# An RWKV-7 and pooling layer on one core: products without a reader, a new order of the first loads, and decayed keys on VectorE

## The chip, the cores and the metric

The kernel runs on one core of one Trainium2 chip. Its engines are TensorE (PE, matrix products; PEld is its weight load), VectorE (DVE), ScalarE (ACT), GpSimd (POOL) and SyncE (SP, which here only issues DMA transfers); each works through its own queue of instructions in order. The metric is the device time of one execution in microseconds, the median of several runs; lower is better. Three runs of the kernel before gave 1648.79, 1649.15 and 1650.57.

## What is computed

One inference step of one layer: 256 new positions of a prompt and 8 sequences of 4 new tokens, 288 columns together, with 2048 channels in float32. In the reference's words, cut:

```python
h = _rmsnorm(x, norm_pre_mix)
z = h @ w_in
zs, zp, zga, zgb = jnp.split(z, ...)
zs_mix = zs + (prev - zs) * mu_shift
ya, new_wkv = _rwkv7_branch(zs_mix, st_wkv, ...)
yb, new_pool = _pool_branch(zp, st_pool, ...)
m = jax.nn.sigmoid(zga) * (ya @ w_branch_a) + jax.nn.sigmoid(zgb) * (yb @ w_branch_b)
x = x + _rmsnorm(m @ w_out, norm_post_mix)
f, new_conv = _conv_ffn(_rmsnorm(x, norm_pre_ffn), st_conv, ...)
x = x + _rmsnorm(f, norm_post_ffn)
# in _rwkv7_branch, per head of 64 channels, per position:
s = s * w_t + sa * b_t + v_t * k_t;   y_t = s @ r_t
```

The recurrence over the positions has 16 heads; its decays w_t, keys k_t and the pair a_t, b_t come from z through small products and nonlinear functions. The outputs are y for both kinds of sequence and the new states (shift, wkv, pool, conv).

## The kernel before, in words

**Layout.** Channels lie on the 128 partitions, the 288 columns on the free axis, so x is 16 slices of 128x288. The big products are made in fp32r with both factors split in two: `scaled_parts` (L354) makes xh on ScalarE (L356) and xl = x·g − xh on VectorE (L357), and each product of a 128x128 block of weights is three matmuls (`three`, L262: whi·xh at L263, whi·xl at L264, wlo·xh at L265).

**The stream of weights.** All weights are cut into units of four blocks (256 KB). SP loads a unit into one of seven `raw` buffers (L187), ScalarE casts it to whi (L202), VectorE subtracts to wlo (L203); whi and wlo have four buffers each. A unit is 12 matmuls. The stream runs through the whole kernel: first the five columns of z with the low-rank inputs and the first branch inputs (`dense_together`, five accumulators over the 16 slices of x side by side, 240 matmuls), then r, k, v, the pooling inputs, the gates and the branch products in an order of stages, then w_out, then the FFN in three thirds.

**The side work.** Between the units, generators do the rest in small steps. Three `Lane` objects each hold a list of them; `advance()` is called at the end of a unit and steps all lanes, `advance(True)` in the middle of a unit and steps lane2 alone. A generator's `yield n` lets n steps pass, and a yielded function is asked at each step until it is true. The 16 heads are done in four groups of two pairs. `front(g)` on lane1 makes a group's decays (cum, eP, eN), AR (the queries, decayed, and the negative keys) and KB (the decayed keys: kq and bb times eN, one multiplication for each and each half of the partitions, L621), and then sets `ready[g]`. `late(g)` on lane2 waits for `ready[g]`, multiplies KB with AR (ps_g), masks the result (Gm), writes a part of it to DRAM and reads it back in another layout (Ab), inverts 32x32 triangles of it on VectorE (`inverse`, from the memset at L725 on), reads the inverse back as W and runs the chain of chunks (ps_x, X, ps_u, UV, ps_s, S). lane3 finishes a group.

**What sets the order.** The instructions of each engine are put in order before the run by a scheduler that simulates the kernel with its own costs; an instruction that is pinned (`pin`) keeps its place among the pinned ones in the order of the program. An engine then works strictly in that order.

**The first microseconds.** ScalarE issues the loads of vec (331 columns of per-channel vectors; the first 16 are the gains g1 of the first norm) and of con (1115 columns of constants: identity, ones, masks, eps). SP issues x in pairs of slices and the first units. `startup()` (L417) on lane1 makes the other 12 slices' parts in pairs and then the squares of x, which POOL adds up (L413), for the first norm. `der` (L447) holds four vectors made from vec.

**The second norm.** `rstd_spread` (L381) sums squares with small products (ps_sum), takes the root on ScalarE and the reciprocal on VectorE, writes it on a diagonal (dg, L392) and spreads it over the partitions with one product (ps_spread, L396). It is called for the norm behind w_out (`rst2`, L1220), whose result scales og; x is updated (L1230) and split into xh and xl for the FFN, which begins right behind it. A second call at the end of the kernel is not touched.

Of the kernel before, what the change touches and what calls it, by code (L numbers as in the profile page):

```python
# [10 lines left out]
F32 = mybir.dt.float32  # L11
# [7 lines left out]
P = 128  # L19
# [22 lines left out]
FA = 2  # L42
TOG = 3
# [64 lines left out]
def hybrid_step(ctx: ExitStack, tc: tile.TileContext, t):  # L108
# [69 lines left out]
    def load_to(u):  # L178
        while cursor["load"] <= min(u, len(units) - 1):
            i = cursor["load"]  # L180
            if i in (4, 4 + 5, 4 + 10):
                x_load((i - 4) // 5 + 1)
            ap, nk = units[i]
            m = ap.shape[2]
            w = wp.tile([P, UK, P], F32, tag="raw", name="raw", bufs=7)
            if i:
                nc.sync.dma_start(out=w[:, :nk, :m], in_=ap)  # L187
            raw[i] = w
            cursor["load"] += 1
# [130 lines left out]
    nc.scalar.dma_start(out=vec, in_=t["vec"])  # L320
# [3 lines left out]
    nc.scalar.dma_start(out=con, in_=t["con"])  # L324
    xr = []

    def x_load(q):
        xq = xr_p.tile([P, 4, N], F32, name=f"xr{q}")
        xr.extend(xq[:, i] for i in range(4))
        if q == 0:  # L330
            load_to(0)
            nc.sync.dma_start(out=xq[:, 0:2], in_=t["xT"][:, 0:2, :])
            nc.sync.dma_start(out=raw[0][:, 0:4], in_=units[0][0][:, 0:4])
            nc.sync.dma_start(out=xq[:, 2:4], in_=t["xT"][:, 2:4, :])
            load_to(1)
        else:
            for h in range(0, 4, 2):
                nc.sync.dma_start(out=xq[:, h:h + 2], in_=t["xT"][:, 4 * q + h:4 * q + h + 2, :])
# [7 lines left out]
    def c_(name):  # L346
        o, w = CON[name]
        return con[:, o:o + w]
# [30 lines left out]
    def rstd_spread(sums, where, between=()):  # L379

        ps = psb.tile([P, 3, 2], F32, tag="s", name="ps_sum")  # L381
        for i, a in enumerate(sums):
            for c in range(3):
                pin(pe.matmul(ps[0:TC, c], a[:, c * TC:(c + 1) * TC], ones[:, 0:2],
                              start=i == 0 and c == 0, stop=i == len(sums) - 1 and c == 2))
            if i < len(between):
                between[i]()
        q = where.tile([TC, 3, 1], F32, tag="rq", name="rq")
# [7 lines left out]
        pin(pe.matmul(pr[:, :N], ones[0:TC], dg.rearrange("p c t -> p (c t)"), start=True, stop=True))  # L396
        return pr[:, :N]
# [6 lines left out]
    def first_parts(k):  # L404
        xh[k], xl[k] = scaled_parts(k, xr[k], v_("g1", k))

    def first_squares(k):
        if k == 0:
            act.activation(out=acc, in_=xr[0], func=AF.Square)
            return  # L410
        sq = xr_p.tile([P, N], F32, tag="sq", name="sq", bufs=3)
        act.activation(out=sq, in_=xr[k], func=AF.Square)
        pool.tensor_tensor(acc, acc, sq, op=ALU.add)  # L413

    def startup():
        for k in range(4, KD, 2):
            first_parts(k)  # L417
            first_parts(k + 1)
            yield
        for k in range(KD):  # L420
            first_squares(k)
            if k % 2:
                yield
        norms["mix"] = rstd_of([acc], "mix", cst)

# [106 lines left out]
    def front(g, rr, kx, vv, lora):  # L532
# [85 lines left out]
        for par in range(2):  # L618
            for eng, src, flip in ((dve, kq, 0), (pool, bb, 1)):
                h, slot = HALF[par], par ^ flip  # L620
                ins = eng.tensor_tensor(  # L621
# [4 lines left out]
                )  # L626
                if eng is dve:
                    pin(ins)
            if not par:
                yield  # L630
# [24 lines left out]
    def late(g):  # L655
# [67 lines left out]
        def inverse():  # L723
            yield 2 * IWAIT
# [270 lines left out]
    act.copy(out=bones_r, in_=c_("bones"))  # L995
# [224 lines left out]
    rst2 = rstd_spread([acc2, sq], ep)  # L1220
# [261 lines left out]
```

## Time and profile before

| | us |
|---|---|
| median of 3 runs | 1649.15 |
| lowest and highest | 1648.79, 1650.57 |
| the profiled execution | 1651.69 |
| its span, first to last instruction | 1649.6 |
| PE busy in it | 1611.8 (98%) |
| DVE, ACT, POOL busy | 1103.4, 816.8, 369.7 |
| PE's mean granted clock | 0.992 of full speed |

The profile is one execution. A row of a timeline has start and length in us, engine, line of the kernel, operation, out<-in by the program's names, shapes and a count, and in brackets the engine's idle time before it with what ended it. Matmuls overlap, so their pace is read from one start to the next, not from a length. A float32 matmul leaves two records, an fp32r one leaves one. Row by row, the starts of PE lie 0.13 us apart for most of the span and 0.24 us apart where the granted clock is half.

### The profile page before, as it was taken

What the parts mean: (1) busy time and instruction counts of PE and PEld (TensorE: products, weight loads), DVE (VectorE), ACT (ScalarE), POOL (GpSimd) and SP (SyncE); (2) the same over time, 40 slices, a digit from 0 to 9 for tenths busy, and PEclk for the clock granted to TensorE, in tenths of its full rate; (3) what the DMA queues carried; (4) which work ended last, traced back from release to release, by engine and by line L of the source; (5) the groups of instructions that cost most, each with busy time, mean ns of one, the idle gap of its engine ahead of it and who ended that gap; (6) DMA issues with size and microseconds to landing.
All of it is one profiled execution on the core that took longest, in us unless ns stands there. A gap on an engine that the chain in (4) does not pass through costs nothing.

```text
span 1649.6 us, 35997 instructions
## 1 busy us (share of the span) xinstructions
PE 1611.8 (98%) x13540; PEld 1577.3 (96%) x13540; DVE 1103.4 (67%) x2217; ACT 816.8 (50%) x1521; POOL 369.7 (22%) x612
## 2 busy tenths in 40 slices
PE   6989999999999999999999999999999999999998
PEld 6989989989989999999899999999999999999998
DVE  6788887888878766645876664446666555666654
ACT  5544445445435445545655554445555433455554
POOL 4574352343332112300211110001111000111111
PEclk9999999999999999999999999999999999999999
DMA  7535546546545648755355555555555555555553
GB/s 241 161 120 165 170 142 200 161 122 190 157 155 181 187 155 288 229 166 190 108 163 167 167 165 167 166 167 165 168 167 166 166 166 167 166 167 167 176 167 108
DMA packets 157230, 278.96 MB, mean 169 GB/s; under 512 B 25584, under 2 KB 32240, under 8 KB 157056
## 3 DMA queue, kind: packets, MB, share of 16 engines
q1 hardware_dynamic: 151104, 259.16, 50.8%
q0 software_dynamic: 5664, 16.77, 2.9%
q8 instruction: 106, 1.74, 0.4%
q10 hardware_dynamic: 288, 0.74, 0.1%
q14 instruction: 68, 0.56, 0.1%
HBM read 262.67 MB, written 13.93 MB: 168 GB/s over the span
## 4 chain that ended last, share of the span: by engine, by line
PE 86%; DVE 4%; DMA 2%; issue 1%; POOL 0%; ACT 0%; SPq 0%; DVEq 0%; POOLq 0%; ACTq 0%
PE acc L265 27%; PE acc L263 27%; PE acc L264 27%; DVE wlo L203 1%; DMA dW<-wt 1%; PE ps_g L671 0%; DVE xl L357 0%; DVE og L1229 0%; PE ps_s L909 0%; DMA W<-dW 0%; PE ps_u L899 0%; PE ps_x L888 0%; PE ps_y L1353 0%; DVE cum L577 0%; DMA raw<-in_w_in 0%
## 5 line engine op out<-in xcount | busy, mean ns | idle before, releaser
L203 DVE TENSOR_TENSOR wlo<-raw,whi 128x512 fp32r<-128x512 f32 x928 | 661.1, 715 | 415.2 <-ACT whi L202 406.7
L202 ACT CAST whi<-raw 128x512 fp32r<-128x512 f32 x928 | 572.0, 620 | 680.6 <-PE acc L264 629.7
L263 PE MATMUL acc<-xh,whi 128*128 128x288 f32 x2736 | 814.3, 298 | 14.5 <-ACT whi L202 8.8
L265 PE MATMUL acc<-xh,wlo 128*128 128x288 f32 x2736 | 811.4, 297 | 7.0 <-DVE wlo L203 7.0
L264 PE MATMUL acc<-xl,whi 128*128 128x288 f32 x2736 | 812.7, 297 | 0.0
L263 PEld LDWEIGHTS acc<-xh,whi 128*128 128x128 f32 x2736 | 517.4, 189 | 17.9 <-ACT whi L202 9.2
L265 PEld LDWEIGHTS acc<-xh,wlo 128*128 128x128 f32 x2736 | 520.2, 190 | 12.0 <-DVE wlo L203 8.9
L264 PEld LDWEIGHTS acc<-xl,whi 128*128 128x128 f32 x2736 | 520.6, 190 | 2.0 <-issue 0.9
L265 PE MATMUL acc<-ah,wlo 128*128 128x288 f32 x704 | 208.7, 296 | 0.0
L263 PE MATMUL acc<-ah,whi 128*128 128x288 f32 x704 | 208.0, 296 | 0.0
L264 PE MATMUL acc<-al,whi 128*128 128x288 f32 x704 | 205.2, 292 | 0.0
L1266 POOL COPY cout<-gt 128x2 f32<-128x2 f32 x44 | 31.1, 706 | 597.2 <-DVE gt L1262 575.9
L264 PEld LDWEIGHTS acc<-al,whi 128*128 128x128 f32 x704 | 134.2, 191 | 0.0
L263 PEld LDWEIGHTS acc<-ah,whi 128*128 128x128 f32 x704 | 132.2, 188 | 0.0
L265 PEld LDWEIGHTS acc<-ah,wlo 128*128 128x128 f32 x704 | 131.9, 187 | 0.0
L1274 POOL TENSOR_TENSOR cv<-cv,rstd_ffn 128x288 f32<-128x288 f32 x44 | 36.2, 823 | 74.5 <-ACT cv L1273 73.6
L732 DVE TENSOR_TENSOR wt<-wt,Ab 128x16 f32<-128x16 f32 (+30 forms) x124 | 51.4, 414 | 1.8
L462 POOL TENSOR_TENSOR df<-zt 128x256 f32<-128x256 f32 (+1 forms) x27 | 22.7, 840 | 91.6 <-DVE zt L460 85.6
L1270 DVE SCALAR_TENSOR_TENSOR cv<-gt,vec,cv 128x255 f32<-128x255 f32 x88 | 43.0, 489 | 0.0
L263 PE MATMUL acc<-ybh,whi 128*128 128x288 f32 x128 | 38.6, 301 | 0.0
L265 PE MATMUL acc<-ybh,wlo 128*128 128x288 f32 x128 | 38.4, 300 | 0.0
L264 PE MATMUL acc<-ybl,whi 128*128 128x288 f32 x128 | 38.1, 298 | 0.0
(308 smaller groups left out, 1539.8 us busy)
## 6 DMA issues: line engine op xcount, KB each, us to landing
raw<-in_w_ffn_in SPq DMA_DIRECT2D x352, 256.0 KB, 3.0
raw<-in_w_in SPq DMA_DIRECT2D x264, 256.0 KB, 3.5
raw<-in_w_ffn_out SPq DMA_DIRECT2D x176, 256.0 KB, 2.7
raw<-in_w_out SPq DMA_DIRECT2D x64, 256.0 KB, 3.0
raw<-in_w_branch_b SPq DMA_DIRECT2D x32, 256.0 KB, 3.2
raw<-in_w_branch_a SPq DMA_DIRECT2D x32, 256.0 KB, 3.9
xr<-in_xT SPq DMA_DIRECT2D x8, 288.0 KB, 5.6
tga<-th POOLq DMA_DIRECT2D x16, 144.0 KB, 3.7
```

The costliest lines, as they stand in the source:

```text
L202: act.copy(out=hi[:, a:b, :m], in_=w[:, a:b, :m])
L203: dve.tensor_tensor(lo[:, a:b, :m], w[:, a:b, :m], hi[:, a:b, :m].bitcast(F32), op=ALU.subtract)
L263: pe.matmul(ps, hi, xh, start=start, stop=False)
L264: pe.matmul(ps, hi, xl, start=False, stop=False)
L265: pe.matmul(ps, lo, xh, start=False, stop=stop)
L462: pool.tensor_tensor(df[:m, :TP], zt[:m, 0:TP], zt[:m, 1:ZB], op=ALU.subtract)
L732: dve.tensor_tensor(tmp[:, :, :n], Wb[:, :, :n], Ab[:, :n, tt].unsqueeze(1).to_broadcast([P, 8, n]), op=ALU.mult)
L1266: pool.tensor_copy(cout[:, f, 0:2], gt[:, TP - 2:TP])
L1270: dve.scalar_tensor_tensor(cv[:, s:TP], gt[:, 0:TP - s], w, cv[:, s:TP], op0=ALU.mult, op1=ALU.add)
L1274: pool.tensor_tensor(cv, cv, rst3, op=ALU.mult)
```

## The change

Four things are done.

*The beginning.* Eleven products of a zeroed 128x128 tile, which nothing reads, stand first on PE. The load of vec brings only its first 16 columns; the rest of it and con are loaded on SP's queue in front of the eighth unit. The first slice of x is loaded alone, before the first unit. `startup()` makes one slice's parts and one slice's square per step, and the squares are pinned, as is the copy of bones.

*The keys.* All four multiplications of KB are on VectorE and pinned, in four steps instead of two, so that `ready[g]` is set two units later.

*The inverse.* Group 0's inverse begins two half steps (one unit) later.

*The second norm.* Five products of constants (ones times the identity, float32, 128 columns) stand behind the sums, and eight behind the spreading product; nothing reads them.

```diff
--- before.py
+++ after.py
@@ -40,6 +40,7 @@
 UK = 4
 AHEAD = 3
 FA = 2
+WARM = 11
 TOG = 3
 BT = 5
 IWAIT = 3
@@ -180,6 +181,9 @@
             i = cursor["load"]
             if i in (4, 4 + 5, 4 + 10):
                 x_load((i - 4) // 5 + 1)
+            if i == 7:
+                nc.sync.dma_start(out=vec[:, KD:], in_=t["vec"][:, KD:])
+                nc.sync.dma_start(out=con, in_=t["con"])
             ap, nk = units[i]
             m = ap.shape[2]
             w = wp.tile([P, UK, P], F32, tag="raw", name="raw", bufs=7)
@@ -317,11 +321,10 @@
     con = cst.tile([P, NCON], F32, name="con")
     xe = ExitStack()
     xr_p = xe.enter_context(tc.tile_pool(name="xr", bufs=1, side="right"))
-    nc.scalar.dma_start(out=vec, in_=t["vec"])
+    nc.scalar.dma_start(out=vec[:, 0:KD], in_=t["vec"][:, 0:KD])
     first = cst.tile([P, 1], F32, name="first")
     dve.memset(first, 0.0)
     act.activation(out=first, in_=first, func=AF.Square)
-    nc.scalar.dma_start(out=con, in_=t["con"])
     xr = []
 
     def x_load(q):
@@ -329,8 +332,9 @@
         xr.extend(xq[:, i] for i in range(4))
         if q == 0:
             load_to(0)
-            nc.sync.dma_start(out=xq[:, 0:2], in_=t["xT"][:, 0:2, :])
+            nc.sync.dma_start(out=xq[:, 0:1], in_=t["xT"][:, 0:1, :])
             nc.sync.dma_start(out=raw[0][:, 0:4], in_=units[0][0][:, 0:4])
+            nc.sync.dma_start(out=xq[:, 1:2], in_=t["xT"][:, 1:2, :])
             nc.sync.dma_start(out=xq[:, 2:4], in_=t["xT"][:, 2:4, :])
             load_to(1)
         else:
@@ -376,7 +380,13 @@
 
     TC = N // 3
 
-    def rstd_spread(sums, where, between=()):
+    def keep_busy(n):
+
+        ps = psb.tile([P, 512], F32, tag="s", name="ps_busy")
+        for _ in range(n):
+            pin(pe.matmul(ps[:, 0:P], ones, ident, start=True, stop=True))
+
+    def rstd_spread(sums, where, between=(), busy=()):
 
         ps = psb.tile([P, 3, 2], F32, tag="s", name="ps_sum")
         for i, a in enumerate(sums):
@@ -385,6 +395,8 @@
                               start=i == 0 and c == 0, stop=i == len(sums) - 1 and c == 2))
             if i < len(between):
                 between[i]()
+        if busy:
+            keep_busy(busy[0])
         q = where.tile([TC, 3, 1], F32, tag="rq", name="rq")
         pin(act.activation(out=q, in_=ps[0:TC, :, 0:1], func=AF.Sqrt, scale=1.0 / D, bias=c_("eps")[0:TC]))
         pin(dve.reciprocal(q, q))
@@ -394,6 +406,8 @@
         ))
         pr = psb.tile([P, 512], F32, tag="s", name="ps_spread")
         pin(pe.matmul(pr[:, :N], ones[0:TC], dg.rearrange("p c t -> p (c t)"), start=True, stop=True))
+        if busy:
+            keep_busy(busy[1])
         return pr[:, :N]
 
 
@@ -406,22 +420,26 @@
 
     def first_squares(k):
         if k == 0:
-            act.activation(out=acc, in_=xr[0], func=AF.Square)
+            pin(act.activation(out=acc, in_=xr[0], func=AF.Square))
             return
         sq = xr_p.tile([P, N], F32, tag="sq", name="sq", bufs=3)
-        act.activation(out=sq, in_=xr[k], func=AF.Square)
+        pin(act.activation(out=sq, in_=xr[k], func=AF.Square))
         pool.tensor_tensor(acc, acc, sq, op=ALU.add)
 
     def startup():
-        for k in range(4, KD, 2):
-            first_parts(k)
-            first_parts(k + 1)
+        for k in range(KD):
+            if k < KD - 4:
+                first_parts(k + 4)
+            first_squares(k)
             yield
-        for k in range(KD):
-            first_squares(k)
-            if k % 2:
-                yield
         norms["mix"] = rstd_of([acc], "mix", cst)
+
+
+    zero = xr_p.tile([P, P], F32, name="zero")
+    pool.memset(zero, 0.0)
+    warm0 = psb.tile([P, 512], F32, tag="s", name="ps_warm")
+    for _ in range(WARM):
+        pin(pe.matmul(warm0[:, :P], zero, zero, start=True, stop=True))
 
     first_parts(0)
     split_to(0)
@@ -615,19 +633,17 @@
         KBs = kp.tile([P, G, 2, 32], F32, tag="KBs", name="KBs")
         rh = kp.tile(W2, F32R, tag="t0", name="rh")
         rl = kp.tile(W2, F32R, tag="t3", name="rl")
-        for par in range(2):
-            for eng, src, flip in ((dve, kq, 0), (pool, bb, 1)):
+        for src, flip in ((kq, 0), (bb, 1)):
+            for par in range(2):
                 h, slot = HALF[par], par ^ flip
-                ins = eng.tensor_tensor(
+                pin(dve.tensor_tensor(
                     KB[h, :, :, slot, :].rearrange("p c g t -> p g c t"),
                     src[h, :, :TP].rearrange("p g (c t) -> p g c t", c=NCH),
                     eN[h, :, :TP].rearrange("p g (c t) -> p g c t", c=NCH),
                     op=ALU.mult,
-                )
-                if eng is dve:
-                    pin(ins)
-            if not par:
-                yield
+                ))
+                if (flip, par) != (1, 1):
+                    yield
         for slot, src in enumerate((kq, bb)):
             pool.tensor_tensor(KBs[:, :, slot, :], src[:, :, TP:], eN[:, :, TP:], op=ALU.mult)
         ready[g] = (vv, AR, KB, KBs, wr, dch, dsm)
@@ -721,7 +737,7 @@
         S0 = kp.tile([P, G, NB, C], F32, tag="S0", name="S0")
         nc.sync.dma_start(out=S0, in_=t["st_wkv"][:, p0:p0 + G])
         def inverse():
-            yield 2 * IWAIT
+            yield 2 * IWAIT + (0 if g else 2)
             pin(dve.memset(Ab.rearrange("p a b -> p (a b)")[:, 0:1024:33], 1.0))
             wt = kp.tile([P, 2, 8, 32], F32, tag="inv", name="wt")
             Wb, tmp = wt[:, 0], wt[:, 1]
@@ -992,7 +1008,7 @@
         lane3.todo.append(finish())
 
     bones_r = zp_.tile([P, P], F32R, name="bones_r")
-    act.copy(out=bones_r, in_=c_("bones"))
+    pin(act.copy(out=bones_r, in_=c_("bones")))
     mB = [dmb.tile([P, N], F32, tag=f"mB{j}", name=f"mB{j}") for j in range(16)]
     tga = [dmb.tile([P, N], F32, tag=f"tga{j}", name=f"tga{j}") for j in range(16)]
 
@@ -1217,7 +1233,7 @@
         act.activation(out=o, in_=ps[:, :N], func=AF.Copy, scale=v_("g2", j))
         og.append(o)
     me.close()
-    rst2 = rstd_spread([acc2, sq], ep)
+    rst2 = rstd_spread([acc2, sq], ep, busy=(5, 8))
     acc3 = ep.tile([P, N], F32, tag="accn3", name="acc3")
     xh, xl = [None] * KD, [None] * KD
```

How this moves the instructions is shown at three places. First VectorE at the start, where xl are the x slices 8 to 15 in their order (L357 before, L361 now) and wlo the weights of the units. Before:

```order
L203 TENSOR_TENSOR wlo<-raw,whi 128x512 x3
L203 TENSOR_TENSOR wlo<-raw,whi 128x4x96
L357 SCALAR_TENSOR_TENSOR xl_233<-xr_111,vec,xh_232 128x288
L357 SCALAR_TENSOR_TENSOR xl_237<-xr_111,vec,xh_236 128x288
L357 SCALAR_TENSOR_TENSOR xl_257<-xr_111,vec,xh_256 128x288
L357 SCALAR_TENSOR_TENSOR xl_261<-xr_111,vec,xh_260 128x288
L357 SCALAR_TENSOR_TENSOR xl_281<-xr_124,vec,xh_280 128x288
L357 SCALAR_TENSOR_TENSOR xl_285<-xr_124,vec,xh_284 128x288
L357 SCALAR_TENSOR_TENSOR xl_305<-xr_124,vec,xh_304 128x288
L357 SCALAR_TENSOR_TENSOR xl_309<-xr_124,vec,xh_308 128x288
L203 TENSOR_TENSOR wlo<-raw,whi 128x512 x4
```

Now:

```order
L207 TENSOR_TENSOR wlo<-raw,whi 128x512
L361 SCALAR_TENSOR_TENSOR xl_291<-xr_113,vec,xh_290 128x288
L361 SCALAR_TENSOR_TENSOR xl_314<-xr_113,vec,xh_313 128x288
L361 SCALAR_TENSOR_TENSOR xl_337<-xr_113,vec,xh_336 128x288
L361 SCALAR_TENSOR_TENSOR xl_362<-xr_113,vec,xh_361 128x288
L207 TENSOR_TENSOR wlo<-raw,whi 128x512 x2
L361 SCALAR_TENSOR_TENSOR xl_387<-xr_126,vec,xh_386 128x288
L361 SCALAR_TENSOR_TENSOR xl_412<-xr_126,vec,xh_411 128x288
L361 SCALAR_TENSOR_TENSOR xl_437<-xr_126,vec,xh_436 128x288
L361 SCALAR_TENSOR_TENSOR xl_462<-xr_126,vec,xh_461 128x288
L207 TENSOR_TENSOR wlo<-raw,whi 128x512
```

Eight xl stood in a row behind four wlo, then four wlo; now two wlo stand behind the first four of the eight xl.

Second VectorE in the second group (g = 1), where AR, KB are made on lane1 (KB at L621 before, L639 now; bb is written on tha) and S and UV belong to the chain of the first group on lane2. Before:

```order
L203 TENSOR_TENSOR wlo<-raw,whi 128x512
L610 TENSOR_TENSOR AR<-rr,eP 128x576
L608 SCALAR_TENSOR_TENSOR AR<-kkr,thw 128x576
L914 TENSOR_TENSOR S<-S,ps_s 128x128
L203 TENSOR_TENSOR wlo<-raw,whi 128x512
L915 TENSOR_TENSOR S<-S,dch 128x128
L203 TENSOR_TENSOR wlo<-raw,whi 128x512
L621 TENSOR_TENSOR KB<-kq,eN 64x2x4x64
L203 TENSOR_TENSOR wlo<-raw,whi 128x512
L621 TENSOR_TENSOR KB<-kq,eN 64x2x4x64
```

Now:

```order
L207 TENSOR_TENSOR wlo<-raw,whi 128x512 x2
L639 TENSOR_TENSOR KB<-kq,eN 64x2x4x64
L930 TENSOR_TENSOR S<-S,ps_s 128x128
L931 TENSOR_TENSOR S<-S,dch 128x128
L207 TENSOR_TENSOR wlo<-raw,whi 128x512
L639 TENSOR_TENSOR KB<-kq,eN 64x2x4x64
L207 TENSOR_TENSOR wlo<-raw,whi 128x512
L858 TENSOR_TENSOR S_1899<-S_1899,ps_st 128x512 x2
L207 TENSOR_TENSOR wlo<-raw,whi 128x512
L639 TENSOR_TENSOR KB<-tha,eN 64x2x4x64
L918 TENSOR_TENSOR UV<-ps_u,wr 64x2x64 x2
L639 TENSOR_TENSOR KB<-tha,eN 64x2x4x64
```

The two halves from bb (KB<-tha) were on POOL and stand on VectorE now, each with a wlo or more in front; the first half from kq stands ahead of S's update, where it stood behind it; AR is made earlier, outside the rows.

Third PE at the second norm. Before:

```order
L265 MATMUL acc<-xh_10011,wlo 128x288
L384 MATMUL ps_sum<-con,acc_10041 96x2 x3
L384 MATMUL ps_sum<-con,sq 96x2 x3
L396 MATMUL ps_spread<-dg,con 128x288
L263 MATMUL acc<-xh_11311,whi 128x288 x6
L264 MATMUL acc<-xl_11312,whi 128x288
L265 MATMUL acc<-xh_11311,wlo 128x288
```

Now:

```order
L269 MATMUL acc<-xh_10027,wlo 128x288
L394 MATMUL ps_sum<-con,acc_10057 96x2 x3
L394 MATMUL ps_sum<-con,sq 96x2 x3
L387 MATMUL ps_busy<-con 128x128 x5
L408 MATMUL ps_spread<-dg,con 128x288
L387 MATMUL ps_busy<-con 128x128 x8
L267 MATMUL acc<-xh_11342,whi 128x288 x6
L268 MATMUL acc<-xl_11343,whi 128x288
L269 MATMUL acc<-xh_11342,wlo 128x288
```

The products of constants stand in the two places between the sums, the spreading product and the FFN's first matmuls; the matmuls behind keep their order.

## The prediction

> **What bounds the kernel now.** I read the page's first part, then what PE waited for, then stretches of the span, then the timelines where PE waited.
>
> ```profile
> span 1649.6 us, 35997 instructions
> PE 1611.8 (98%) x13540; PEld 1577.3 (96%) x13540; DVE 1103.4 (67%) x2217; ACT 816.8 (50%) x1521; POOL 369.7 (22%) x612
> ```
>
> ```profile
> PE acc L263 <- ACT whi L202: 8.8, 1, 8.8
> PE acc L265 <- DVE wlo L203: 7.6, 6, 3.3
> PE acc L263 <- DVE zb L1027: 4.1, 1, 4.1
> PE ps_u L899 <- ACT X L894: 2.8, 1, 2.8
> ...
> PE acc L263 <- ACT xh L356: 1.6, 1, 1.6
> PE acc L263 <- ACT dh L363: 1.4, 1, 1.4
> PE ps_x L888 <- DVE S L915: 1.3, 1, 1.3
> PE ps_s L909 <- DVE UV L902: 1.2, 1, 1.2
> PE ps_spread L396 <- DVE dg L392: 1.0, 1, 1.0
> ```
>
> ```profile
> 100.00:150.00 50.00, 43.66 (x366) 41.73 (x365) 40.81 (x97) 22.35 (x45) 35.91 (x57) 0.90 0.51 146
> 350.00:480.00 130.00, 123.13 (x1284) 116.05 (x1284) 111.84 (x258) 59.89 (x122) 55.77 (x88) 0.97 0.51 155
> 860.00:1649.00 789.00, 785.12 (x5906) 782.08 (x5904) 453.70 (x840) 384.66 (x663) 80.27 (x136) 1.00 0.53 164
> ```
>
> TensorE is the bound: it is idle for 1649.6 − 1611.8 = 37.8 us, and the columns of the second fence (sum, times, longest, us) say on what. In the third fence the columns are busy time of PE, PEld, DVE, ACT and POOL, then PE's granted clock; the last 789 us lose nothing and are not touched. Besides idle time PE loses clock: 0.90 over 50 us is 10 us at half speed. So whatever the change can win is in the waits above and in the slow time behind them; the rest is product after product.
>
> **The beginning.** Timelines of PE, ACT, DVE and POOL, and of the DMA view of the first 20 us the rate in slices of 0.5 us and con's issue (KB, us to landing):
>
> ```profile
> 8.83 0.61 PE L263 MATMUL acc<-xh,whi 128*128 128x288 f32 x1 [8.83 <-ACT whi L202]
> ...
> 12.27 0.30 PE L263 MATMUL acc<-xh,whi 128*128 128x288 f32 x1
> ...
> 25.54 0.29 PE L264 MATMUL acc<-xl,whi 128*128 128x288 f32 x1
> 29.14 0.47 PE L265 MATMUL acc<-xh,wlo 128*128 128x288 f32 x1 [3.30 <-DVE wlo L203]
> ...
> 49.75 0.29 PE L265 MATMUL acc<-xh,wlo 128*128 128x288 f32 x1
> ```
>
> ```profile
> 8.16 0.62 ACT L202 CAST whi<-raw 128x512 fp32r<-128x512 f32 x1 [2.22 <-DMA raw<-in_w_in]
> ```
>
> ```profile
> GB/s 0 0 0 55 96 267 339 300 231 220 213 285 371 399 424 372 363 343 362 385 382 406 386 386 394 389 352 355 384 376 388 415 378 384 400 383 390 369 164 107
> ...
> con<-in_con ACTq DMA_DIRECT2D x1, 557.5 KB, 7.5
> ```
>
> ```profile
> 21.68 6.80 DVE L357 SCALAR_TENSOR_TENSOR xl<-xr,vec,xh 128x288 fp32r<-128x288 f32 x8
> 28.40 2.48 DVE L203 TENSOR_TENSOR wlo<-raw,whi 128x512 fp32r<-128x512 f32 x4
> ```
>
> The clock's two speeds, read where PE changes from one to the other behind the second norm:
>
> ```profile
> 791.96 1.81 PE L263 MATMUL acc<-xh,whi 128*128 128x288 f32 x6 [1.61 <-ACT xh L356]
> 793.57 0.44 PE L264 MATMUL acc<-xl,whi 128*128 128x288 f32 x1
> 793.81 0.44 PE L265 MATMUL acc<-xh,wlo 128*128 128x288 f32 x1
> ...
> 797.64 0.29 PE L264 MATMUL acc<-xl,whi 128*128 128x288 f32 x1
> ```
>
> A product starts 0.24 us after the last at half clock; at full clock 789.00 us hold 5906 of them, 0.13 each: 0.11 lost on each slow one. The first 8.83 to 12.27 are at half clock: 3.44 / 0.24 = 14 products, 1.5 us lost. The 240 products of the first stage end at 49.9. Since 240 at 0.132 are 31.7, this stage spends 18.2 us on other things: 8.8 before the first product, 1.5 of clock, 3.3 of waiting for wlo, 1.5 of clock again behind it, and 3.1 of shorter waits.
>
> What goes: con's 557.5 KB and most of vec no longer stand in front of the first weights. The first product needs 147 KB of x and one 256 KB unit, 0.4 MB, and the queues move 220 to 340 GB/s from 2.5 us on: landed about 4.0 to 4.8, plus the cast of 0.62. The eleven products of zeros are bounded by the transposes L697 (8 records for 4 of them, each 128 columns of f32):
>
> ```profile
> 120.18 1.09 PE L697 MATMUL ps_t<-con,KB 128*128 128x128 f32 x8
> 121.03 0.38 PE L264 MATMUL acc<-xl,whi 128*128 128x288 f32 x1
> ```
>
> 0.85 / 4 = 0.21 each at full clock, twice that at half: started in the first 0.4 to 1.2 us they end between 5.0 and 5.8. First real product: 5.4, so 3.4 earlier, and at full clock: 1.5 more. The eight xl in a row (0.85 each) stand in front of the four wlo at 28.40; in the new order two wlo stand between two fours of xl, so I expect the 3.3 and its clock loss (1.5) to go, of the shorter waits nothing, and 0.7 to come anew from weights not landed yet: 3.3 + 1.5 − 0.7 = 4.1. **Term 1: 3.4 + 1.5 + 4.1 = 9.0**; ends: 3.4 (start alone) and 11.5 (3.4 + 1.5 + 4.8, and 1.8 of the shorter waits). What is late next is der: it waits on VectorE for the rest of vec, behind seven weight units on SP's queue. 3.1 MB at 385 GB/s put that at 10 to 11 us, and four xl and four wlo are ahead of it; at 14 it would stall the fifth wlo, inside the lower end. The two DMAs are issued by SP right ahead of the eighth unit, which is wanted only after 84 products; the squares and the copy of bones, pinned now, run on ScalarE, busy 816.8 of 1649.6. I cost both at nothing; without that cover an issue or a square would be 0.4 us.
>
> On the clock, the Trainium skill ("TensorE: Matmul & The Clock Gate", Part 1) says that a free-running window of about 3.4 us must be busy, and that its phase is not tied to the kernel. The trace agrees with the length: 12.27 − 8.83 = 3.44. By that rule eleven products can end before the window does, and up to 9 real products would still be slow, an estimate of 1.0 us off this term.
>
> **The keys' halves.** VectorE and POOL beside each other, columns start and length:
>
> ```profile
> 233.45 3.48 POOL L621 TENSOR_TENSOR KB<-tha,eN 64x512 f32<-64x512 f32 x2
> ```
>
> ```profile
> 101.41 1.98 DVE L203 TENSOR_TENSOR wlo<-raw,whi 128x512 fp32r<-128x512 f32 x2
> 103.42 1.64 DVE L621 TENSOR_TENSOR KB<-kq,eN 64x512 f32<-64x512 f32 x1
> ...
> 234.22 1.58 DVE L203 TENSOR_TENSOR wlo<-raw,whi 128x512 fp32r<-128x512 f32 x1
> 235.72 1.35 DVE L915 TENSOR_TENSOR S<-S,dch 128x128 f32<-128x128 f32 x1
> 237.00 0.68 DVE L203 TENSOR_TENSOR wlo<-raw,whi 128x512 fp32r<-128x512 f32 x1
> ...
> 357.56 0.68 DVE L621 TENSOR_TENSOR KB<-kq,eN 64x512 f32<-64x512 f32 x1
> 358.47 1.95 DVE L621 TENSOR_TENSOR KB<-kq,eN 64x512 f32<-64x512 f32 x1
> 360.46 1.73 DVE L608 SCALAR_TENSOR_TENSOR AR<-kkr,thw 128x576 f32<-128x576 f32 x1
> ...
> 453.25 1.76 DVE L203 TENSOR_TENSOR wlo<-raw,whi 128x512 fp32r<-128x512 f32 x1
> ```
>
> While POOL multiplies its two halves (3.48), VectorE's wlo takes 1.58 where it takes 0.68 alone, KB 1.95 instead of 0.68. Each of the four groups has such a place, and PE's waits stand right behind. Moving two halves costs VectorE 2 × 0.68 a group and takes the stretching away. By place:
> - 101: wlo 1.98 − 1.36 and KB 1.64 − 0.68 give 1.6 back; the 4.1 wait becomes 2.5. Rows ahead of zb are the same as before. Slow clock follows it for two windows (10 us at half in 100 to 150, three windows of 3.4 us, one of them from the wait at 144); I count a little less than one of the two as gone, 1.3: 2.9.
> - 235: 0.90 and about 1.07 of stretching go, one KB (0.68) now stands ahead of S: 1.3 (all of the wait, 1.3, for 1.29).
> - 362 and 369: 1.27 + 1.0 go, 1.36 comes: 0.9.
> - 454: 1.1 on wlo, 0.5 on others go, one KB comes: 1.0 of the 2.8 wait; clock 0.97 over 130 us is two windows, 2.7 us of products; half of it: 2.3 together.
>
> **Term 2: 7.4**; ends 0 (the added halves take it all back) and 14.0 (waits and clock all gone).
>
> The Trainium skill ("SBUF — State Buffer", section "SBUF: two separate sides") speaks against the price of 0.68: the pair of ports is held for a whole instruction by whichever of VectorE and GpSimd starts first, so a half placed beside what POOL still does would wait for it. The row at 358.47 agrees (1.95). With all eight added halves at 1.95, the term would be 7.4 − 8 × 1.27, below zero; that is the slower rival below.
>
> **Products added beside the second norm; inverse.** PE waits 1.0 for dg, then 1.6 for xh, then runs at 0.24 from 791.96 to 797.3: 22 products. Five products are 5 × 0.21 = 1.06, eight are 1.70: they fill both waits and add about 0.1. **Term 3: 22 × 0.11 − 0.2 = 2.2**; ends 0 (one short idle stretch is enough to lose the clock) and 2.4. The cover is complete: were dg 1 us earlier, they would cost that. Group 0's inverse one unit (12 products, 1.58 us) later has VectorE wait less at its memset, behind which dh and the 1.4 wait stand, with a slow window behind (1.5). But the order has seven wlo between the last Gm and the memset both times, so the memset comes little later against the transfer it waits for. **Term 4: 0.6**, ends −1 and 2.9. Its late end is covered: 53 products (7 us) are left between the lane's last work and its first use.
>
> **Term 5: −3.0.** ready comes two units later, and the stream's order differs at every group: two new waits of the size of those quoted (1.2 to 1.6); ends −6 and 0.
>
> **Sum.** 9.0 + 7.4 + 2.2 + 0.6 − 3.0 = 16.2. The profiled execution took 1651.69 (span 1649.6 and 2.1 around it), so 1635.5; the median of the three runs is 2.5 below that execution: **1633**.
>
> **Rivals.**
> - *The beginning gives only its earlier start* (0.15): weights do not land fast enough, the waits return a few units on. For: the queues move over 340 GB/s from 6 us on, without a pause; against: con's bytes are out of that stretch. 16.2 − 5.6: 1638.5.
> - *The middle gives nothing* (0.15): VectorE is at 111.84 of 130 in 350 to 480 and pays with its own time. 9.0 + 2.2: 1638. With the first, 5.6: 1643.5.
> - *Slower* (0.06): VectorE becomes the engine waited for in all four groups. Eight added halves at 1.95 are 15.6, and each group loses another slow window, 4 × 1.5 = 6: 21.6 against 11.2 from terms 1 and 3, +10.4: 1659.5. It decides from 14.5 us lost, 3.6 a group. Against: the longest row is 1.95 with POOL's halves beside it, and these go.
> - *Nothing* (0.06): the planner's order puts new waits for 11 to 16 us in the place of the gain, or the clock drops at the start as before: 1649.
> - *My forecast's terms* (0.58): 1627 to 1640 is its own range.
>
> Range 1624 to 1645: the low end is terms 1 to 4 near their upper halves (25), the high end both of the first rivals together. A change below 0.2% (3.3 us) can't be told from none. Faster 0.88, same 0.06, slower 0.06.
>
> **What would show it.** First real product at 5 to 6 with 0.13 between starts; the 240th by 39 to 42; no wlo above 1 us in the four groups' places and no wait for S at 235, moved by the gain so far; zb's wait 2.5 or less; 0.13 between starts right behind the second norm; the last 789 us as before. I am wrong if the first stage ends behind 45, or if PE's wait for VectorE between 90 and 470 is not below the 18 or so of now.

## The result, and the profile after

The changed kernel takes 1636.84 us (median of 4 runs, 1634.78 to 1640.18); the kernel before, on the same chip, 1649.86 (1648.79 to 1651.35). The ratio is 0.9922 with a 95% interval of 0.9903 to 0.9942: 13 us faster, between 10 and 16. The forecast was 1633, range 1624 to 1645. The execution profiled took 1636.18, 15.5 less than the one profiled before.

The page's first part, after:

```profile
span 1634.4 us, 36105 instructions
PE 1612.8 (99%) x13588; PEld 1577.4 (97%) x13588; DVE 1101.7 (67%) x2225; ACT 817.1 (50%) x1521; POOL 350.6 (21%) x605
```

PE is busy 1.0 us longer, for 48 records more (24 products without a reader), and idle 21.6 us where it was 37.8. VectorE has eight multiplications more and is busy 1.7 us less: the stretching that POOL's halves caused is gone, though other work of POOL still stretches VectorE (a wlo of 2.45 at 447.75). What PE waits for now (us in total, times, longest):

```profile
PE ps_q L874 <- DVE tq L868: 3.3, 3, 1.6
PE acc L269 <- DVE wlo L207: 3.3, 5, 1.3
PE acc L267 <- DVE zb L1043: 2.8, 1, 2.8
PE acc L267 <- DVE gt L1278: 2.0, 1, 2.0
PE acc L267 <- DVE ybl L1090: 2.0, 1, 2.0
```

The waits for X, S, UV, dg and xh are gone and the one for zb is 2.8 where it was 4.1; the ones for gt and ybl are new.

Where the time went is seen best from the big products themselves: both kernels make the same 11136 of them (tile acc), so the start of the n-th in the trace before less the start of the n-th in another trace is that kernel's lead there, in us. Where the granted clock is half, for a window of 3.4 us or several, I say that PE runs at half clock. Worked out from the rows of the traces, for the changed kernel and four of the experiments below:

| n | start before | changed | beginning alone | keys alone | POOL's halves, 3 pauses | VectorE, 1 pause |
|---|---|---|---|---|---|---|
| 1 | 8.83 | 2.6 | 2.3 | 0.9 | 2.6 | 2.6 |
| 240 | 49.75 | 6.8 | 6.7 | -0.9 | 7.0 | 7.3 |
| 400 | 72.11 | 4.6 | 3.4 | -0.9 | 4.9 | 5.0 |
| 500 | 86.13 | 4.6 | 3.4 | -0.9 | 4.9 | 5.0 |
| 900 | 159.87 | 7.7 | 4.3 | 0.1 | 6.3 | 5.3 |
| 1200 | 204.48 | 10.3 | 4.3 | 3.0 | 8.6 | 4.5 |
| 2000 | 347.31 | 6.9 | 4.1 | -2.0 | 6.6 | -2.9 |
| 2500 | 432.38 | 8.9 | 3.4 | -1.1 | 7.0 | 0.1 |
| 2700 | 477.25 | 15.6 | 9.1 | 5.3 | 14.6 | 3.8 |
| 4700 | 773.42 | 15.5 | 8.9 | 3.8 | 13.5 | 3.7 |
| 4850 | 800.94 | 17.6 | 9.3 | 3.9 | 15.6 | 5.8 |
| 5050 | 829.14 | 19.4 | 8.6 | 5.7 | 17.3 | 7.6 |
| 5200 | 849.08 | 15.1 | 8.6 | 4.7 | 14.6 | 4.8 |
| 11136 | 1634.03 | 15.1 | 8.6 | 4.7 | 14.6 | 4.8 |

Each column is one execution, and executions of one kernel differ by up to 7 us (see the last section), so differences of a few us between columns are not read as results; the medians are. In the changed kernel the beginning gives 6.8 and loses 2.2 of it again by the 400th product, the middle gives 10.9, the second norm 2.1 and the rows behind it 1.8, and the FFN's first gates take 4.3 back. The middle's gain is waits and clock together. Between 90 and 470 us PE waited 16.4 us before and 9.6 now, and ran at half clock for 17.1 us before (from 104.4, 145.4 and 456.0 on) and for 3.4 now (from 337.5 on). The 13.7 us less at half clock are some 6 us (57 products at 0.11, an estimate).

### The profile page after: what moved, and what is told of

It reads as the page before. It is cut to its first block, busy times and chain, and to the rows that moved or that the text cites. A ratio compares the mean times of both kernels' runs of the same rounds, so it can differ in the third digit from the quotient of the medians.

```text
span 1634.4 us, 36105 instructions
## 1 busy us (share of the span) xinstructions
PE 1612.8 (99%) x13588; PEld 1577.4 (97%) x13588; DVE 1101.7 (67%) x2225; ACT 817.1 (50%) x1521; POOL 350.6 (21%) x605
## 4 chain that ended last, share of the span: by engine, by line
PE 90%; DVE 5%; issue 1%; DMA 1%; POOL 1%; ACT 0%; SPq 0%; DVEq 0%; POOLq 0%; ACTq 0%
PE acc L267 28%; PE acc L269 28%; PE acc L268 28%; DVE wlo L207 2%; DVE wt L748 1%; PE ps_g L687 1%; DMA dW<-wt 0%; DVE wt L751 0%; PE ps_s L925 0%; PE ps_u L915 0%; PE ps_y L1369 0%; PE ps_x L904 0%; PE ps_v L723 0%; PE ps_x L905 0%; PE ps_sl L835 0%
## 5 line engine op out<-in xcount | busy, mean ns | idle before, releaser
L1286 DVE SCALAR_TENSOR_TENSOR cv<-gt,vec,cv 128x255 f32<-128x255 f32 (+1 forms) x88 | 43.4, 494 | 0.3 <-ACT cv L1279 0.3
```

The source lines that it names most:

```text
L1286: dve.scalar_tensor_tensor(cv[:, s:TP], gt[:, 0:TP - s], w, cv[:, s:TP], op0=ALU.mult, op1=ALU.add)
```

## The experiments

Each ran in five rounds; a ratio is to the kernel before, run beside it, with its 95% interval.

**1. The beginning alone.** The changed kernel with the other parts undone (of the keys' loops the first lines alone, the words behind # added):

```diff
-        for src, flip in ((kq, 0), (bb, 1)):   # four steps, all on dve
+        for par in range(2):                   # kq on dve, bb on pool, one pause
-            yield 2 * IWAIT + (0 if g else 2)
+            yield 2 * IWAIT
-    rst2 = rstd_spread([acc2, sq], ep, busy=(5, 8))
+    rst2 = rstd_spread([acc2, sq], ep)
```

> The beginning alone (products of zeros, load order, one slice per step), without the keys on VectorE, the later inverse and the products beside the second norm. Theory from the two traces: the 240th product comes 6.8 us earlier as in the changed kernel and about 2 us of that are given back by the 400th, so 4.6 us in all, 1645. Rival, the forecast: 9 us, 1640.5. If it gives under 3.3 the beginning is worth nothing that can be measured.

Measured: 1642.61, 0.9954 (0.9941 to 0.9966): 7.6 us, between the two. The 240th product leads by 6.7. Of the table's 8.6 at the end, 5.8 came between the 2500th and the 2700th: the wait for X at 454 (2.8 before) is down to 0.4 here too, with POOL's halves in place. That is a change of order, not of the engines.

**2. The products beside the second norm alone.** The kernel before with `keep_busy` as in the change and this call:

```diff
-    rst2 = rstd_spread([acc2, sq], ep)
+    rst2 = rstd_spread([acc2, sq], ep, busy=(5, 8))
```

> The kernel before with the five and eight products beside the second norm alone; the order up to that norm is the one of before. Theory from the traces: 2.1 us are won behind the norm (full clock at once) and lost again at the FFN's first gates, where three wlo now stand ahead of gt on VectorE (a wait of 2.0 us with a slow window of 1.5 behind it): between 1649 and 1651, no gain. Rival, the forecast's third term: 2.2 us stay, 1647.5.

Measured: 1649.31, 0.9999 (0.9991 to 1.0008). No gain, as the theory from the traces had it. In its execution 2.1 us of lead come between the 4700th and the 4850th product, and PE waits 2.0 us for gt, as in the changed kernel.

**3. The changed kernel without them.**

```diff
-    rst2 = rstd_spread([acc2, sq], ep, busy=(5, 8))
+    rst2 = rstd_spread([acc2, sq], ep)
```

> The changed kernel without the five and eight products beside the second norm; the order up to the norm is the changed kernel's. Theory: the slow stretch of 2.1 us behind the norm comes back, the wait for gt of 2.0 us goes with its slow window, the sum is nothing: 1636 to 1637, the same as the changed kernel. Rival, the forecast's third term: 2.2 us slower, 1639.

Measured: 1634.41, 0.9911 (0.9897 to 0.9924): not slower than with them. Both runs say the part is worth nothing as it stands. Why is in the timelines of the changed kernel, PE behind the norm and at the first gates:

```profile
774.70 1.95 PE L387 MATMUL ps_busy<-con 128*128 128x128 f32 x16
776.47 1.06 PE L267 MATMUL acc<-xh,whi 128*128 128x288 f32 x6
777.55 0.40 PE L268 MATMUL acc<-xl,whi 128*128 128x288 f32 x1
777.79 0.29 PE L269 MATMUL acc<-xh,wlo 128*128 128x288 f32 x1
777.92 0.30 PE L268 MATMUL acc<-xl,whi 128*128 128x288 f32 x1
...
817.60 0.37 PE L267 MATMUL acc<-xh,whi 128*128 128x288 f32 x1 [2.00 <-DVE gt L1278]
```

and VectorE at those gates, now and then before:

```profile
813.39 1.95 DVE L378 RECIPROCAL rstd_ffn<-rstd_ffn 128x288 f32<-128x288 f32 x1 [0.20 <-ACT rstd_ffn L377]
815.26 1.82 DVE L207 TENSOR_TENSOR wlo<-raw,whi 128x512 fp32r<-128x512 f32 x3
817.00 0.81 DVE L1278 TENSOR_TENSOR gt<-acc,rstd_ffn 128x288 f32<-128x288 f32 x2
```

```profile
827.06 1.95 DVE L374 RECIPROCAL rstd_ffn<-rstd_ffn 128x288 f32<-128x288 f32 x1
830.53 0.46 DVE L1262 TENSOR_TENSOR gt<-acc,rstd_ffn 128x288 f32<-128x288 f32 x1 [1.52 <-PE acc L265]
```

Behind the norm PE runs at 0.13 at once, as forecast (the 2.1 of the table). But with the thirteen products the scheduler puts the FFN's norm product 40 places later (behind 267 of the stage's products, where without them, in run 3, it stands behind 227) and three wlo between the reciprocal and gt. I take it that it counts the thirteen as PE time. Before, gt waited for PE; now PE waits 2.0 us for gt, and a window of half clock follows.

**4. The keys alone.**

```diff
-            for eng, src, flip in ((dve, kq, 0), (pool, bb, 1)):
+        for src, flip in ((kq, 0), (bb, 1)):
+            for par in range(2):
...
+                if (flip, par) != (1, 1):
+                    yield
```

> The kernel before with the decayed keys on VectorE in four steps alone. Theory: the middle's gain (10.9 us between the 500th and the 4700th product in the traces) is mostly this part's, because POOL's long multiplications beside VectorE are gone: 8 to 11 us, 1639 to 1642. Rival, the forecast's terms two, four and five: 5 us, 1645. Rival of those who hold that VectorE only takes over the work: no gain, 1650.

Measured: 1640.08, 0.9945 (0.9932 to 0.9959): 9 us, the first theory's size. But this part changes two things, the engine and the pauses (each `yield` between two halves is one), and the next runs separate them. (The execution profiled took 1646.7, 6.7 above the median; its column in the table is low for that.)

**5. POOL's halves back, pauses kept.** Two halves on POOL as before, three pauses as in the change:

```diff
-                pin(dve.tensor_tensor(
+                ins = (pool if flip else dve).tensor_tensor(
...
+                if not flip:
+                    pin(ins)
```

> The changed kernel with the two halves from bb back on POOL, still in four steps; PE's order differs from the changed kernel's by a few products only. Theory, the two engines stretch each other: VectorE's rows beside POOL's halves take 1.3 to 2 us again, 5 to 9 us slower than the changed kernel, 1642 to 1646. Rival, the order: what wins the middle is that ready comes later and rows stand elsewhere (the beginning alone removed the wait of 3.0 us at 454 too): within 2 us of the changed kernel, 1635 to 1639.

Measured: 1638.36, 0.9930 (0.9916 to 0.9944). The rival holds: 1.5 us from the changed kernel, not to be told apart, and far from 5 to 9. Yet the stretching is there, in the first group's rows of VectorE and POOL:

```profile
98.78 1.64 DVE L639 TENSOR_TENSOR KB<-kq,eN 64x512 f32<-64x512 f32 x1
```

```profile
96.50 3.37 POOL L639 TENSOR_TENSOR KB<-tha,eN 64x512 f32<-64x512 f32 x2
```

KB takes 1.64 beside POOL and 0.70 in the changed kernel at the same place, and the two wlo in front of it 2.35 against 1.40: 1.9 together. Behind them stands zb, for which PE waits 4.6 against 2.8:

```profile
PE acc L267 <- DVE zb L1045: 5.3, 2, 4.6
```

So each stretch is real, but it reaches PE in the first group alone: in the other three KB takes up to 1.16, 1.77 and 1.78, and the list of this run's waits has none for S, X or UV above 0.4.

**9. VectorE's halves, one pause.**

```diff
-                if (flip, par) != (1, 1):
+                if (flip, par) == (0, 1):
                     yield
```

> The changed kernel with all four halves on VectorE but in two half steps with one pause, as before, so that ready comes two units earlier. Theory after the run with POOL's halves in four steps, the order wins: without the pauses most of the middle's gain beyond the engine's 1.5 us goes, 1640 to 1643. Rival, the engine wins: 1636 to 1638.

Measured: 1646.66, 0.9989 (0.9980 to 0.9997): 11 us slower than the changed kernel, and slower than either expected. With runs 1, 5 and the changed kernel this makes four corners (run 1 also lacks two parts that runs 2 and 10 find to be worth nothing):

| ratio to before | bb's halves on POOL | all on VectorE |
|---|---|---|
| one pause | 0.9954 (0.9941 to 0.9966) | 0.9989 (0.9980 to 0.9997) |
| three pauses | 0.9930 (0.9916 to 0.9944) | 0.9922 (0.9903 to 0.9942) |

With one pause, moving the halves to VectorE costs 0.0035, 6 us; the intervals are apart. With three pauses the engine makes no difference that is measured. The pauses are worth 0.0067, 11 us, on VectorE; with the halves on POOL they come out at 0.0024, 4 us, with intervals that overlap, so nothing is shown there. What they do: `ready` is set two units later and the halves are spread, so that one KB stands between two wlo; with one pause two KB come in a row,

```profile
231.70 1.38 DVE L639 TENSOR_TENSOR KB<-tha,eN 64x512 f32<-64x512 f32 x2
241.16 1.40 DVE L639 TENSOR_TENSOR KB<-kq,eN 64x512 f32<-64x512 f32 x2
```

and the later work of the lanes meets the stream elsewhere. (bb's halves, written second, come first here: so the pinned instructions of an engine are not all kept in the order of the program, as the words on the kernel before have it. What holds them these runs do not show.) What PE waits for there:

```profile
PE acc L267 <- DVE zb L1043: 6.5, 2, 4.5
PE ps_q L874 <- DVE tq L868: 4.7, 5, 1.9
```

Between the 1700th and the 2000th product that kernel loses 7.5 us of lead, at a wait for tq at 318 and the half clock behind it, while the KB of that group come at 354. So the largest single loss lies where no KB is. Which of the two, the spread or the later `ready`, does it, these runs do not separate; they show that the placing is worth 11 us on VectorE, and that the engine by itself wins nothing.

**6. One and four products.** The scheduler's order flips back to the 227th product if few products are added:

```diff
-    rst2 = rstd_spread([acc2, sq], ep, busy=(5, 8))
+    rst2 = rstd_spread([acc2, sq], ep, busy=(1, 4))
```

> The changed kernel with one product behind the sums and four behind the spreading product in place of five and eight. With these the first norm product of the FFN stands at the 5027th product instead of the 5067th, and gt right behind the reciprocal. Theory: if one and four products keep the clock, the 2.1 us behind the norm stay and the wait for gt goes, 2 to 3 us faster than the changed kernel, 1633 to 1634.5. Rival: too little work, the clock drops, as without any: 1634.5 to 1636.

Measured: 1635.15, 0.9913 (0.9896 to 0.9929). In the execution profiled the clock holds with two idle stretches of 0.71 left:

```profile
772.19 0.75 PE L408 MATMUL ps_spread<-dg,con 96*128 96x288 f32 x2 [0.71 <-DVE dg L404]
772.78 1.06 PE L387 MATMUL ps_busy<-con 128*128 128x128 f32 x8
774.55 1.06 PE L267 MATMUL acc<-xh,whi 128*128 128x288 f32 x6 [0.71 <-ACT xh L360]
```

and there is no wait for gt, but a wait of 1.1 for whi at 787 comes in its place. The interval covers the changed kernel and run 3: nothing gained for sure.

**7. One and eight, and the FFN's squares earlier.**

```diff
             second_parts(k)
+            second_squares(k - 4)
...
-            for k in range(KD):
+            for k in range(KD - 4, KD):
                 second_squares(k)
...
-    rst2 = rstd_spread([acc2, sq], ep, busy=(5, 8))
+    rst2 = rstd_spread([acc2, sq], ep, busy=(1, 8))
```

> The changed kernel with one and eight products beside the second norm and each FFN square made four slices behind its parts instead of all behind the last; the norm product stands at the 5029th. Theory: clock kept and no wait for gt, 1632 to 1634. Rival: the squares between the parts make xl late on VectorE and PE waits there: 1636 or above.

Measured: 1634.69, 0.9908 (0.9894 to 0.9923), the best ratio of all, by 0.0014 under the changed kernel and inside its interval; the time is above the theory's 1632 to 1634. No wait for gt. In the execution profiled one product in front was too few: the window's PE was busy 2.33 of 3.50 us and the next ran at half clock (columns: busy PE, PEld, DVE, ACT, POOL, then the granted clock):

```profile
768.90:772.40 3.50, 2.33 (x19) 1.95 (x19) 1.50 (x4) 1.41 (x4) 0.00 (x0) 1.00 0.46 161
772.40:775.80 3.40, 3.40 (x19) 3.40 (x18) 3.33 (x9) 2.02 (x5) 1.34 (x2) 0.50 0.00 0
```

**8. con and vec early again.**

```diff
-            if i == 7:
-                nc.sync.dma_start(out=vec[:, KD:], in_=t["vec"][:, KD:])
-                nc.sync.dma_start(out=con, in_=t["con"])
-    nc.scalar.dma_start(out=vec[:, 0:KD], in_=t["vec"][:, 0:KD])
+    nc.scalar.dma_start(out=vec, in_=t["vec"])
+    nc.scalar.dma_start(out=con, in_=t["con"])
```

> The changed kernel with vec whole and con loaded by ScalarE at once, as before; everything else changed. Theory, the loads' order makes the early start: the first real product comes at 7.5 to 9 us and the 240th 2 to 4 us later than in the changed kernel, 1639 to 1641. Rival: the engines set it (the slices' parts and casts), no difference, 1636 to 1637.

Measured: 1644.05, 0.9961 (0.9946 to 0.9975), 6 us slower than the changed kernel; more than the theory's 2 to 4. ScalarE's first cast and PE's first product:

```profile
7.23 0.62 ACT L203 CAST whi<-raw 128x512 fp32r<-128x512 f32 x1 [2.84 <-DMA raw<-in_w_in]
```

```profile
7.90 0.61 PE L264 MATMUL acc<-xh,whi 128*128 128x288 f32 x1 [2.57 <-ACT whi L203]
```

The loads' order sets the start. In this execution the lead at the 240th product is 4.0 where the changed kernel has 6.8, so the order is worth 2.8 there, as the theory had it; the rest of the 6 us is lost further on (the last lead is 7.1 against 15.1), where the stream meets the lanes' work elsewhere. With con early, what is left of the beginning adds nothing measurable to the keys alone (0.9961 against 0.9945). One slice per step was not tried alone.

**10. Without the later inverse.**

```diff
-            yield 2 * IWAIT + (0 if g else 2)
+            yield 2 * IWAIT
```

> The changed kernel without the later inverse of the first group. Forecast's fourth term: 0.6 us slower, not to be told from none, 1636 to 1638. Rival: the order around it decides, as for the keys, and the wait of 1.7 us with its slow window near 143 returns: 3 us slower, 1640.

Measured: 1636.10, 0.9928 (0.9914 to 0.9942): no difference.

**11. Without the products of zeros.**

```diff
-    for _ in range(WARM):
-        pin(pe.matmul(warm0[:, :P], zero, zero, start=True, stop=True))
```

> The changed kernel without the eleven products of zeros. Theory: the first real product comes at the same time (its data set it), the first 14 products run at half clock: 1.5 us slower, 1638 to 1639. Rival: the first products wait for their parts anyway, and the slow window hides there: no difference, 1636 to 1637.

Measured: 1635.68, 0.9918 (0.9905 to 0.9932): no difference. The first products do run at half clock without them, with 0.24 us or more between their starts up to 11.96, and they start at about the same time as in the changed kernel (6.27):

```profile
6.11 0.61 PE L267 MATMUL acc<-xh,whi 128*128 128x288 f32 x1 [6.11 <-ACT whi L206]
```

In that execution the lead at the 50th product is 1.5 where the changed kernel has 2.3, and 3.2 in both at the 100th: the slow products hide in waits for weights that come anyway. Nor do the eleven keep the clock in every execution: in those of runs 1, 7 and 8 it fell again for a window or two from 8.67, 7.84 and 7.81 on.

**12. The first norm earlier as well.** Run 7 and the last four squares of the first norm without pauses:

```diff
             first_squares(k)
-            yield
+            if k < KD - 4:
+                yield
+        yield
```

> The changed kernel with one and eight products beside the second norm, the FFN's squares four slices behind their parts, and the first norm's last squares without pauses between them, so that the first norm's product stands at the 201st product instead of the 214th. Theory: what the changed kernel gives back between the 240th and the 400th product (2.2 us) is the late first norm; half of it stays: 1632.5 to 1634. Rival: the waits there come from the split of weights, no gain over the kernel with early FFN squares alone (0.9908 of before).

Measured: 1634.49, 0.9917 (0.9903 to 0.9930): no gain over run 7, and the lead at the 400th product is 5.0, against 5.2 in run 7. The norm product comes 2.0 us earlier than in the changed kernel, and the root on ScalarE 1.2 earlier. PE's waits for zwa_h and zt (0.7 and 0.3 in the changed kernel) are gone, and two waits for wlo, 1.0 and 0.8, stand in their place, as the rival had it.

## Why the prediction was right, and where its steps were not

The direction, the sum's size (16.2 forecast, 13 measured, 15.5 between the two executions profiled) and the range held. The terms did not all: errors of both signs lie in the sum, so that it came out so near is in part luck. Of the signs it named, some were missed by little: the first product at 6.3 and not 5 to 6, the 240th at 43.0 and not 39 to 42, the wait for zb 2.8 and not 2.5, and a wlo of 2.45 in the fourth group's place. Its 18 us of waiting for VectorE between 90 and 470 is a misreading: the rows give 12.2, and 16.4 with the waits for ScalarE; now it is 9.6.

**Term 1, the beginning, 9.0: mis-sized.** The lead at the 240th product is 6.8, and 4.6 at the 400th; alone it measures 7.6 (5.6 to 9.7), with some of that from the later order. ScalarE's first cast, and PE:

```profile
5.60 0.62 ACT L206 CAST whi<-raw 128x512 fp32r<-128x512 f32 x1 [1.84 <-DMA raw<-in_w_in]
```

```profile
1.00 5.06 PE L442 MATMUL ps_warm<-zero 128*128 128x128 f32 x22 [1.00 <-POOL zero L439]
6.27 0.44 PE L267 MATMUL acc<-xh,whi 128*128 128x288 f32 x1 [0.21 <-ACT whi L206]
...
28.69 0.40 PE L269 MATMUL acc<-xh,wlo 128*128 128x288 f32 x1 [1.29 <-DVE wlo L207]
```

The first unit landed at 5.6, not at 4.0 to 4.8, so the first product came 2.6 earlier, not 3.4; why it landed later stays open (the prediction's own 0.4 MB at 220 to 340 GB/s from 2.5 us on give 3.7 to 4.4). The wait of 3.3 became 1.3 and no slow window follows it; I had it gone, with 0.7 elsewhere. The 1.5 for the clock of the first 14 products was not there to win: run 11, without the eleven products, measured no difference.

**What is late next: the wrong transfer.** I named der; it does not wait (VectorE makes it at 14.33 with no idle time in front). ScalarE, SP and VectorE now:

```profile
40.69 0.41 ACT L367 CAST lo_h<-lora 128x256 fp32r<-128x256 f32 x1 [2.19 <-DMA lora<-in_lora]
41.12 1.28 ACT L377 ACT_TABLE_LOAD   x1
42.41 0.50 ACT L377 ACTIVATE rstd_mix<-ps_rstd,con 128x288 f32<-128x288 f32 x1
```

```profile
36.74 0.78 SPq L1019 DMA_DIRECT2D lora<-in_lora  x1
```

```profile
42.95 1.95 DVE L378 RECIPROCAL rstd_mix<-rstd_mix 128x288 f32<-128x288 f32 x1 [1.39 <-ACT rstd_mix L377]
```

and SP and VectorE before:

```profile
31.29 0.42 SPq L1003 DMA_DIRECT2D lora<-in_lora  x1
```

```profile
43.93 1.95 DVE L374 RECIPROCAL rstd_mix<-rstd_mix 128x288 f32<-128x288 f32 x1 [1.12 <-ACT rstd_mix L373]
```

PE is 6.8 us ahead there, but the load of lora is issued 5.4 us later than before, because SP's queue has 26 units in front of it where it had 19; the copy of lora stands on ScalarE ahead of the root, and so the first norm is only 1.0 us earlier. 2.2 us of lead go between the 240th and the 400th product: 0.7 and 0.3 of them are PE's waits for the norm's first users (zwa_h and zt), 0.4 is a wait for wlo, and the rest is no wait that the profile shows. That lora holds back more than this is not shown: in run 12, with the root 1.2 us earlier, waits for wlo took the place, and an earlier load of lora was not tried.

**Term 2, the keys, 7.4: the mechanism failed.** The step that failed is "each of the four groups has such a place, and PE's waits stand right behind": I gave those waits to the stretching, place by place. The four corners give the engine nothing measurable with three pauses, and a loss of 6 us with one; there the rival "the middle gives nothing, VectorE pays with its own time" was right. What wins, with the halves on VectorE, is the placing, which term 5 had as a cost of 3.0 and no gain. Terms 2, 4 and 5 together were 5.0. In the medians the keys' part is worth 5.3 on top of the beginning (0.9954 to 0.9922, with intervals that just touch) and 9 alone; the 10.9 of the middle in the profiled execution holds the wait for X at 454 too, which went with the beginning alone (run 1). So the size of the three terms was met without their mechanism, which is luck. What the Trainium skill ("SBUF — State Buffer", section "SBUF: two separate sides") says of the ports that VectorE and GpSimd share agrees with these rows, KB at 1.64 beside POOL and 0.70 alone. But a longer row is not a longer kernel.

**Term 3, the second norm, 2.2: right place, wrong sum.** 2.1 were won behind the norm, and lost at the gates 40 us on; alone the part is worth 0.2 (-1.3 to 1.5 us). The step that failed is "the cover is complete": the two waits did cover the products, but the order changed as if they took time (run 2, from the kernel before: the norm product 45 places later, and the same wait for gt). The rows to see it stood in the order, three wlo between the reciprocal and gt.

**Term 4, the inverse, 0.6:** nothing measurable, as forecast. **Term 5, -3.0:** the new waits are there (2.0 for ybl at 110, 2.0 for gt, tq's longest 0.8 grown to 1.6); the one for gt is the second norm's (run 2), and the others came with the gain.

**The rivals.** "Only the earlier start" did not come; "slower" was near in run 9, where VectorE takes the halves without the pauses and loses nearly all that the beginning won.

## What to carry to other kernels

In a kernel whose instruction order is made by a scheduler, an edit is worth what it does to the order: cost the rows it moves far from the edit before the rows it shortens, and separate "another engine" from "another time" by a run for each corner. Work that fills an idle wait can still cost where the scheduler moves other rows for it. When the first engine comes forward, ask for every transfer ahead of the next joint result (here lora, ahead of the norm's root), not only for the one that was moved.

## What the runs showed of the hardware that was not expected

**The clock falls without an idle PE.** In the changed kernel's execution, with PE busy throughout by the profile (timeline of PE, then stretches; the number behind POOL's is the granted clock):

```profile
82.91 1.23 PE L576 MATMUL ps_n<-con,sq 64*64 64x2 f32 x29
...
85.08 0.44 PE L268 MATMUL acc<-xl,whi 128*128 128x288 f32 x1
85.33 0.44 PE L269 MATMUL acc<-xh,wlo 128*128 128x288 f32 x1
```

```profile
81.40:84.90 3.50, 3.50 (x51) 3.15 (x50) 2.62 (x5) 1.40 (x3) 3.34 (x6) 1.00 0.44 124
84.90:88.30 3.40, 3.40 (x18) 3.11 (x17) 3.23 (x13) 0.95 (x2) 2.83 (x3) 0.50 0.33 114
```

Some 1.3 us of products with two columns each (36 of them, ps_n) fill PE's rows, and the window behind runs at half clock. That they count as little work is the reading I have; nothing was run on it.

**The same rows, another clock.** Run 3 has the same order up to the second norm, and the same stretch in its execution:

```profile
81.30:84.80 3.50, 3.50 (x50) 3.15 (x49) 2.62 (x5) 1.40 (x3) 3.34 (x6) 1.00 0.40 128
84.80:88.20 3.40, 3.40 (x29) 3.22 (x28) 3.23 (x13) 1.10 (x3) 2.83 (x3) 1.00 0.32 110
```

It keeps the full clock where the changed kernel lost it. The Trainium skill ("TensorE: Matmul & The Clock Gate", Part 1) says that the window of about 3.4 us is free-running and does not start anew with the kernel. The traces agree: within each of them the clock changes at whole multiples of 3.41 us from its first change, and where these edges lie differs from trace to trace. The changed kernel's execution changes at 6.39 and 84.90, so that ps_n, which starts between 82.91 and 84.24, lies within one window, 81.49 to 84.90. Run 3's changes at 4.45 and 100.02, so that an edge at 82.96 falls among the same products.

The same 36 products stand in all 14 executions profiled. In six of them (the changed kernel and runs 2, 5, 6, 10 and 11) the clock falls right behind, and each time all 36 lie within one window. In the eight others it does not: in five an edge falls among them, and in three (runs 1, 4 and 12) they begin or end within 0.3 us of one. So on the same rows it goes with the place of the edges.

That this makes the spread between executions is argued, not shown. The changed kernel's lie 5.4 us apart, the slowest with a mean granted clock of 0.993 and the others with 0.996 and 0.997; those of the keys alone lie 7.4 apart (1639.35 to 1646.74), the two slowest with 0.991 and the others with 0.993 to 0.996. A difference of 2 us needs many executions here, and one profile's places of half clock are not the kernel's.
